# Token halves of 512 and 520 instead of 516 and 516 in a seven-product matrix scheme

## The chip, the core and the metric

The kernel runs on one core of a Trainium2 chip. The metric is device time in microseconds from start to end of one execution. The core has a matrix engine (TensorE, PE in the profile), three engines for elementwise work (VectorE, DVE; ScalarE, ACT; GpSimd, POOL) and a queue engine that issues transfers (SyncE, SP). Matmul results go to PSUM, eight banks of 512 fp32 numbers per partition, from which VectorE or ScalarE takes them.

## The reference

One layer of a decoder trunk for 1024 prompt tokens and 8 sample tokens that share the weights, 1032 tokens in all, width 1024:

```python
x = x + concat(pool_mixer(a), conv_mixer(glu)) @ w_out
x = x + cross_attn(rmsnorm(x, g_attn), mk, mv, w_q, w_o)
h = rmsnorm(x, g_ffn)
x = x + (silu(h @ w_gate) * (h @ w_up)) @ w_down      # D_FF = 2816, 22 tiles of 128
```

and a final RMSNorm; the state of the pooling and of the convolution and the memory's keys and values go out too. The change is about the third line, the SwiGLU.

## The kernel before, in words

All tensors lie with channels on the 128 partitions and tokens along the free dimension: 512 even prompt tokens, 512 odd ones, then 8 samples. fp32 matmuls are made of three passes over a high and a low part of each operand (`PASSES`, `split`).

The two matrix products of the SwiGLU are done by a scheme with seven block products in place of eight. Its blocks halve the tokens, the input channels and the output channels. The token halves are `TH` = 516 wide. For stage one (`first_two`, `sixth`, `others`) the blocks A11, A12, A22 of the normalised input and the sums S1 to S4 are made once (`plain_block`, `sum_blocks`) and kept as `ab`; for each of 22 hidden tiles f the weights' blocks and sums are prepared (`gu_load`, `gate_prep`, `sums_prep`: tiles wG, wTa, wTb, wU) and seven products of 4 blocks x 3 passes follow, in this order: A11 and A12 with wG, S2 in between with wTa, S3 with wTa, S1 and A22 with wTb, S4 with wU. VectorE (A11: ScalarE) adds each product from PSUM into the four quarters of `su` (`plus`, `copy_sums`); S1's is added twice, the second time after A22's. Multiplying by the row factors `Rf`, the SiLU and the blocks of the hidden activations for stage two (`gated`, `times_value`, `combine`, `to_blocks`, stored in the DRAM buffer `hb`) follow.

Stage two is the down projection: for each of the blocks A11, S2, S3, S1, A22, A12, S4 four units (`p`), each a product of 11 hidden pairs x 3 passes (`down_block`, `down_weights`, `whole_unit`, `first_half_unit`); the last unit is cut into two column spans (`LAST_SPANS`, `last_units`, line 1647), so that the final norm of one can run under the other.

`product` (line 1287) issues the matmuls. Each block product is two matmuls per weight block, 258 columns each (`TQ`), and takes a place in PSUM: products number 0 and 1 of every three take two banks of a three-bank buffer (`mm`, two of them), number 2 takes two single-bank buffers (`ms`, two of them).

What sets the order of all this is `Program.order`: a list planner with a cost per task and engine, priorities in program order, and buffers that are given out as they come free. It fixes each engine's instruction list when the kernel is built; on the chip each engine goes through its list in order and waits where an operand or a buffer is not ready. Tasks with a choice of engine (`{"Pool": ..., "DVE": ...}`) are placed by it too.

Of the kernel before, what the change touches and what calls it, by code (L numbers as in the profile page):

```python
# [49 lines left out]
LAST_SPANS = ((516, 516), (0, 258), (258, 258))  # L50
# [196 lines left out]
def hybrid_step_kernel(ctx: ExitStack, tc: tile.TileContext, io):  # L247
# [228 lines left out]
    def rsqrt_rows(name, dst, dkeys, total, tkeys, ones, lo, width, at=None, more=None, direct=False):  # L476
# [12 lines left out]
        for o, n in parts:  # L489
# [6 lines left out]
            if direct:  # L496
# [296 lines left out]
    def windows(g):  # L793
# [86 lines left out]
    def layer_norm():  # L880
        y_all = [conv_keys(cg) for cg in range(4)]
        for o, n in SPANS:
            ps = ms_buf(f"mean_ps{o}")
            add({"PE": 0.1 + 0.0017 * n}, lambda e, ps=ps, o=o, n=n: e.matmul(ps[:, :n], ones_c, ysum[:, o : o + n], start=True, stop=True),
                [(ysum,)], [(ps,)])
            for cg in range(4):
                add({"DVE": dve(n)}, lambda e, cg=cg, ps=ps, o=o, n=n: e.tensor_tensor(
                    y2[cg // 2][:, cg % 2, o : o + n], y2[cg // 2][:, cg % 2, o : o + n], ps[:, :n], ALU.subtract),
                    [(ps,)] + y_all[cg], [("yc", cg, o)])
# [308 lines left out]
    def quarter(j, i, h):  # L1198
        return xa[j][:, i, h * TH : (h + 1) * TH]

    def plain_block(b, j, i, h):
        split(lambda p: block(b, j, p), lambda p: bkey(b, j, p), lambda: quarter(j, i, h), TH, [(xa[j], i, h)], gain=vcol(V_FFN, j + 4 * i))
# [84 lines left out]
    def product(weights, wkeys, xs, steps=1):  # L1287
# [11 lines left out]
        def bank(c):  # L1299
            return sums[0][0]()[:, c] if len(sums) == 1 else sums[c][0]()  # L1300

        def emit(e, js):
            for j in js:
                for p, (wi, xi) in enumerate(PASSES):
                    for c in range(2):
                        e.matmul(bank(c), weights(j, wi), xs[0](j, xi)[:, c * TQ : (c + 1) * TQ],  # L1306
                                 start=j == 0 and p == 0, stop=j == nj - 1 and p == 2)
# [7 lines left out]
    def from_sums(sums, engine, cost, emit, r, w):  # L1315
        for src, sl, key in sums:
            add({engine: cost(sl.stop - sl.start)}, lambda e, src=src, sl=sl: emit(e, src(), sl), [key] + r, w)

    def plus_sums(o, okey, a, akey, sums):

        from_sums(sums, "DVE", dve, lambda e, src, sl: e.tensor_tensor(as_banks(o(sl), src), src, as_banks(a(sl), src), ALU.add),  # L1321
                  [akey], [okey])
# [470 lines left out]
```

## Time and profile before

| | |
|---|---|
| Time, median of 3 runs | 1245.13 us (1244.81 to 1248.44) |
| Time of the profiled execution | 1247.23 us |
| Its span, first to last instruction | 1245.4 us, mean granted TensorE clock 0.991 |
| TensorE busy | 1207.4 us, 8892 matmuls |
| VectorE, ScalarE, GpSimd busy | 934.3, 500.5, 429.3 us |
| Output projection of the attention ends, stage one begins | about 556 us |
| Down projection begins | about 1008 us |

The profile gives one execution. A row of the page or of a view names line, engine, operation, out<-in, partitions x columns, count, busy time and mean length, and the idle time of the engine just before with what ended it. The length of a matmul is longer than its distance to the next, since matmuls overlap; the distance is what counts. "L1306" is the matmul of `product`, "L1321" the sum out of PSUM.

### The profile page before, as it was taken

What the parts mean: (1) busy time and instruction counts of PE and PEld (TensorE: products, weight loads), DVE (VectorE), ACT (ScalarE), POOL (GpSimd) and SP (SyncE); (2) the same over time, 40 slices, a digit from 0 to 9 for tenths busy, and PEclk for the clock granted to TensorE, in tenths of its full rate; (3) what the DMA queues carried; (4) which work ended last, traced back from release to release, by engine and by line L of the source; (5) the groups of instructions that cost most, each with busy time, mean ns of one, the idle gap of its engine ahead of it and who ended that gap; (6) DMA issues with size and microseconds to landing.
All of it is one profiled execution on the core that took longest, in us unless ns stands there. A gap on an engine that the chain in (4) does not pass through costs nothing.

```text
span 1245.4 us, 22115 instructions
## 1 busy us (share of the span) xinstructions
PE 1207.4 (97%) x8892; PEld 1187.1 (95%) x8892; DVE 934.3 (75%) x1510; ACT 500.5 (40%) x677; POOL 429.3 (34%) x375
## 2 busy tenths in 40 slices
PE   8999996999999989999999999999999999999996
PEld 8999985999999979998999999999999999999996
DVE  7899888757367786669997878878887687656653
ACT  6766658454223452444222222222222243334531
POOL 3578741022101002214544353334353333345100
PEclk9999997999999999999999999999999999999998
DMA  7447686744256664233554546454533498554632
GB/s 282 104 85 165 143 241 174 215 96 153 102 181 226 239 236 170 102 107 97 179 166 141 172 161 197 146 170 153 183 120 111 134 336 306 202 195 152 177 114 69
DMA packets 102422, 208.74 MB, mean 168 GB/s; under 512 B 10096, under 2 KB 53296, under 8 KB 101040
## 3 DMA queue, kind: packets, MB, share of 16 engines
q1 hardware_dynamic: 98720, 194.23, 46.1%
q0 software_dynamic: 3600, 13.11, 6.1%
q8 instruction: 70, 1.15, 0.4%
q14 instruction: 32, 0.26, 0.1%
HBM read 159.75 MB, written 47.55 MB: 166 GB/s over the span
## 4 chain that ended last, share of the span: by engine, by line
PE 74%; DVE 10%; issue 7%; DMA 5%; ACT 2%; POOL 2%; SPq 0%; DVEq 0%; POOLq 0%; ACTq 0%
PE pr L1306 46%; PE ps L460 12%; PE oa L460 4%; PE ob L460 4%; DVE cacc L679 2%; DMA raw<-in_w_v 2%; PE sc L1016 2%; PE pv L1074 2%; PE fd L1647 1%; DMA gr<-in_w_gu 1%; DVE su L1321 1%; POOL w L363 1%; DVE su L1347 1%; PE psg L460 1%; PE psv L460 1%
## 5 line engine op out<-in xcount | busy, mean ns | idle before, releaser
L1306 PE MATMUL pr<-hb,dw 128*128 128x258 f32 x1716 | 208.7, 284 | 0.0
L1306 PEld LDWEIGHTS pr<-hb,dw 128*128 128x128 f32 x1716 | 207.8, 190 | 0.2
L1321 DVE TENSOR_TENSOR su<-pr,su 128x258 f32<-128x258 f32 (+1 forms) x204 | 109.5, 557 | 64.5 <-PE pr L1306 63.2
L1306 PE MATMUL pr<-ab,wG 128*128 128x258 f32 x1056 | 134.4, 283 | 2.6 <-DVE su L1321 1.8
L1306 PE MATMUL pr<-ab,wTa 128*128 128x258 f32 x1056 | 134.0, 283 | 0.0
L1306 PEld LDWEIGHTS pr<-ab,wG 128*128 128x128 f32 x1056 | 129.8, 189 | 3.4 <-ACT wU L352 2.4
L1306 PE MATMUL pr<-ab,wTb 128*128 128x258 f32 x1056 | 130.8, 283 | 1.1 <-DVE su L1321 1.1
L1306 PEld LDWEIGHTS pr<-ab,wTa 128*128 128x128 f32 x1056 | 130.1, 189 | 0.0
L1306 PEld LDWEIGHTS pr<-ab,wTb 128*128 128x128 f32 x1056 | 128.6, 190 | 1.3 <-DVE su L1321 1.3
L460 PE MATMUL ps<-xop,w 128*128 128x344 f32 x720 | 114.1, 320 | 0.5 <-DMA w<-in_w_in 0.5
L460 PEld LDWEIGHTS ps<-xop,w 128*128 128x128 f32 x720 | 113.3, 188 | 0.7 <-DMA w<-in_w_in 0.7
L460 PE MATMUL ps<-xq,w 128*128 128x344 f32 x576 | 94.8, 321 | 0.0
L460 PE MATMUL po<-oo,w 128*128 128x344 f32 x576 | 91.0, 320 | 0.4 <-DVE oo L1079 0.4
L460 PEld LDWEIGHTS po<-oo,w 128*128 128x128 f32 x576 | 90.7, 188 | 0.7 <-DVE oo L1079 0.7
L460 PEld LDWEIGHTS ps<-xq,w 128*128 128x128 f32 x576 | 90.7, 188 | 0.1
L679 DVE SCALAR_TENSOR_TENSOR cacc<-glu,vec,cacc 128x511 f32<-128x511 f32 (+14 forms) x116 | 77.0, 740 | 0.0
L352 ACT ACTIVATE wTa<-ta 128x1024 fp32r<-128x1024 f32 x22 | 23.4, 1064 | 110.9 <-DVE ta L1265 98.6
L1306 PE MATMUL pr<-ab,wU 128*128 128x258 f32 x528 | 67.1, 283 | 0.0
L352 ACT ACTIVATE dw<-dr 128x1024 fp32r<-128x1024 f32 (+1 forms) x36 | 33.0, 923 | 82.6 <-PE pr L1306 72.3
L1306 PEld LDWEIGHTS pr<-ab,wU 128*128 128x128 f32 x528 | 65.0, 190 | 0.0
L352 ACT ACTIVATE w<-raw 128x1024 fp32r<-128x1024 f32 (+2 forms) x32 | 29.4, 922 | 86.4 <-issue 38.6
L1347 DVE TENSOR_TENSOR su<-su,Rf 128x516 f32<-128x516 f32 x73 | 62.8, 863 | 1.5 <-ACT su L1354 0.6
(301 smaller groups left out, 2132.3 us busy)
## 6 DMA issues: line engine op xcount, KB each, us to landing
gr<-in_w_gu SPq DMA_DIRECT2D x44, 512.0 KB, 4.0
hs<-hb SPq DMA_DIRECT2D x35, 516.0 KB, 5.2
hb<-su SPq DMA_DIRECT2D x11, 1032.0 KB, 5.0
ds<-in_w_dn SPq DMA_DIRECT2D x22, 512.0 KB, 3.4
td<-ds SPq DMA_DIRECT2D x88, 128.0 KB, 2.1
dr<-td SPq DMA_DIRECT2D x16, 704.0 KB, 5.4
dr<-in_w_dn SPq DMA_DIRECT2D x24, 320.0 KB, 5.0
spcache_k<-in_cache_k SPq DMA_DIRECT2D x12, 512.0 KB, 4.8
```

Source lines behind the costliest of these rows:

```text
L352: e.activation(dst(0), src(), AF.Copy, scale=1.0 if gain is None else gain)
L363: e.tensor_tensor(dst(1), src(), f32(dst(0)), ALU.subtract)
L460: e.matmul(ps[:, c, :CW], w[:, wi, cols], x[:, xi, c * CW : (c + 1) * CW], start=first and p == 0, stop=last and p == 2)
L679: e.scalar_tensor_tensor(acc[h][:, n:], src[:, : HALF - n], w, acc[h][:, n:], ALU.mult, ALU.add)
L1016: e.matmul(bank()[:, i * NMEM : (i + 1) * NMEM], qop[2 * h + dt][:, qi, tt * P : (tt + 1) * P], kk[:, ki, 2 * (h % 2) + dt], start=(dt == ...
L1074: e.matmul(ps[:, c], v[:, vi, m, col : col + P], pT[h][m][:, pi, sl], start=(m == 0 and p == 0), stop=(m == 1 and p == 2))
L1306: e.matmul(bank(c), weights(j, wi), xs[0](j, xi)[:, c * TQ : (c + 1) * TQ], start=j == 0 and p == 0, stop=j == nj - 1 and p == 2)
L1321: from_sums(sums, "DVE", dve, lambda e, src, sl: e.tensor_tensor(as_banks(o(sl), src), src, as_banks(a(sl), src), ALU.add), [akey], [okey])
L1347: add({"Pool": pool_tt(TH), "DVE": dve(TH)}, lambda e: e.tensor_tensor(o(), o(), b(), ALU.mult), r + [(su[f], q)], [(su[f], q)], lock=True)
L1647: e.matmul(view(), weights(j, wi), moving(j, xi)[:, sl], start=j == 0 and n == 0, stop=j == PAIRS - 1 and n == 2)
```

## The change

The token halves become 512 and 520 wide: the first holds the even prompt tokens, the second the odd ones and the 8 samples. Blocks that hold only the first half (A11, A12, and S4, whose samples would be nothing) are 512 wide, the others (A22, S1, S2, S3) 520. A 512-wide product is one matmul per weight block into one single-bank buffer (`ms`); a 520-wide one is two of 260 into a three-bank buffer (`mm`). The ring of three places is gone: the width decides. Sums of blocks run over 512 columns, and the 8 samples' columns, which the first half does not have, are handled apart: cleared (`no_samples`), negated (`negate`), or split from S1 (S2's samples). The planner's costs for the two kinds of product are new. The transfers to and from `hb` are 512 or 520 columns wide. `LAST_SPANS` becomes (512, 520), (0, 256), (256, 256).

For the longer rows, memory is taken from two small tiles: `ones_c` (1/512) is dropped, the convolution's norm uses `ones_d` (1/1024) with a factor of -2 or `of=2`, and the sample scores `ssc` share the buffer `cnt`, so that `s_scores` comes after the pooling's `mean`.

```diff
-LAST_SPANS = ((516, 516), (0, 258), (258, 258))
+LAST_SPANS = ((512, 520), (0, 256), (256, 256))
...
-TH = T // 2
-TQ = TH // 2
+HALF_AT, HALF_WIDTH = (0, SEQ // 2), (SEQ // 2, SEQ // 2 + NS)
+TW = HALF_WIDTH[1]
 A12, A22, S4, S1, A11, S2, S3 = range(7)
+WIDTH = {A12: HALF_WIDTH[0], S4: HALF_WIDTH[0], A11: HALF_WIDTH[0], A22: TW, S1: TW, S2: TW, S3: TW}
...
-    ssc = const.tile([P, HEADS, 2, NS], F32, name="ssc")
+    ssc = cnt
...
-                    y2[cg // 2][:, cg % 2, o : o + n], y2[cg // 2][:, cg % 2, o : o + n], ps[:, :n], ALU.subtract),
+                    y2[cg // 2][:, cg % 2, o : o + n], ps[:, :n], -2.0, y2[cg // 2][:, cg % 2, o : o + n], ALU.mult, ALU.add),
...
+        split(lambda p: block(S2, j, p)[:, HALF_WIDTH[0] :], lambda p: bkey(S2, j, p) + ("samples",),
+              lambda: whole(S1)()[:, HALF_WIDTH[0] :], NS, [key(S1)], gain=-1.0)
...
-    def product(weights, wkeys, xs, steps=1):
+    def product(weights, wkeys, xs, width, steps=1):
...
-        if i % 3 < 2:
-            t = mm_buf(f"pr{i}", 2)
-            sums = [(lambda: t[:, :, :TQ], slice(0, TH), (t,))]
-        else:
-            sums = [(lambda t=t: t[:, :TQ], slice(c * TQ, (c + 1) * TQ), (t,)) for c, t in enumerate([ms_buf(f"pr{i}_{c}") for c in range(2)])]
...
+        banks = 1 if width <= 512 else 2
+        n = width // banks
+        t = mm_buf(f"pr{i}", 2) if banks == 2 else ms_buf(f"pr{i}")
+        sums = (t, width, n)
 
         def emit(e, js):
             for j in js:
                 for p, (wi, xi) in enumerate(PASSES):
-                    for c in range(2):
-                        e.matmul(bank(c), weights(j, wi), xs[0](j, xi)[:, c * TQ : (c + 1) * TQ],
+                    for c in range(banks):
+                        e.matmul(t[:, c, :n] if banks == 2 else t[:, :n], weights(j, wi), xs[0](j, xi)[:, c * n : (c + 1) * n],
                                  start=j == 0 and p == 0, stop=j == nj - 1 and p == 2)
...
-            add({"PE": 0.1195 * 6 * len(js)}, lambda e, js=js: emit(e, js),
-                wkeys + [k for j in js for k in xs[1][j]], [k for _, _, k in sums])
+            add({"PE": (0.231 if banks == 1 else 0.242) * 3 * len(js)}, lambda e, js=js: emit(e, js),
+                wkeys + [k for j in js for k in xs[1][j]], [(t,)])
...
+    def no_samples(o, okeys):
+        add({"Pool": 0.08}, lambda e: e.memset(o(), 0.0), [], okeys)
...
+            if negate:
+                e.tensor_scalar(o(tail), b(tail), -1.0, 1.0, ALU.mult, ALU.mult)
```

The planner's lists change with it. TensorE where stage one begins, before, from the last matmul of the output projection (`po7`); `pr` is a product's place in PSUM, with the product's number in program order (`pr0` and `pr1` are A11 and A12 of tile 0, `pr4` and `pr5` its S2 and S3), `ab4`, `ab0` and `ab5` are A11, A12 and S2, `Rf_ps` are the column sums for the row factors, which read the sum of squares `xss2`:

```order
L460 MATMUL po7_5134<-oo7_4405,w52_5046 128x344 x9
L1306 MATMUL pr0_5237<-ab4_0_4637,wG0_5144 128x258 x12
L1306 MATMUL pr0_5237<-ab4_1_4972,wG0_5144 128x258 x6
L1306 MATMUL pr1_5267<-ab0_0_4681,wG0_5144 128x258 x12
L1306 MATMUL pr0_5237<-ab4_1_4972,wG0_5144 128x258 x6
L1306 MATMUL pr1_5267<-ab0_1_5062,wG0_5144 128x258 x6
L491 MATMUL Rf_ps0_5300<-xss2_4628,ones_d_72 128x512
L491 MATMUL Rf_ps512_5305<-xss2_4628,ones_d_72 128x512
L491 MATMUL Rf_ps1024_5310<-xss2_4628,ones_d_72 128x8
L1306 MATMUL pr1_5267<-ab0_1_5062,wG0_5144 128x258 x6
L1306 MATMUL pr4_5326<-ab5_0_4744,wTa0_5208 128x258 x12
L1306 MATMUL pr4_5326<-ab5_1_5156,wTa0_5208 128x258 x6
```

The same place in the changed kernel:

```order
L459 MATMUL po7_5138<-oo7_4402,w52_5049 128x344 x9
L1315 MATMUL pr4_5247<-ab5_0_4738,wTa0_5214 128x260 x12
L1315 MATMUL pr4_5247<-ab5_1_5160,wTa0_5214 128x260 x6
L490 MATMUL Rf_ps0_5283<-xss2_4625,ones_d_72 128x512
L490 MATMUL Rf_ps512_5288<-xss2_4625,ones_d_72 128x512
L490 MATMUL Rf_ps1024_5293<-xss2_4625,ones_d_72 128x8
L1315 MATMUL pr0_5298<-ab4_0_4634,wG0_5148 128x512 x6
L1315 MATMUL pr0_5298<-ab4_1_4995,wG0_5148 128x512 x6
L1315 MATMUL pr1_5324<-ab0_0_4678,wG0_5148 128x512 x6
L1315 MATMUL pr1_5324<-ab0_1_5065,wG0_5148 128x512 x6
L1315 MATMUL pr4_5247<-ab5_1_5160,wTa0_5214 128x260 x6
L1315 MATMUL pr5_5356<-ab6_0_4741,wTa0_5214 128x260 x12
```

18 matmuls of S2 stand ahead of the factor sums, where 42 of A11 and A12 stood.

VectorE in tile 14 of stage one, before, from the sum of S2 (`pr99`) on; `pr100` is A12's product, `pr101` S3's (two single banks), `pr102` S1's, `pr103` A22's; `ds` belongs to the down projection's weights, `gr`, `ta`, `tb` to the next tiles' weights:

```order
L1321 TENSOR_TENSOR su14_8639<-pr99_8611,su14_8639 128x516
L1321 TENSOR_TENSOR su14_8639<-pr100_8647,su14_8639 128x516
L1347 TENSOR_TENSOR su14_8639<-su14_8639,Rf_5342 128x516
L363 TENSOR_TENSOR wG15_8705<-gr15_0_8375,wG15_8705 128x1024
L1347 TENSOR_TENSOR su14_8639<-su14_8639,Rf_5342 128x516
L1321 TENSOR_TENSOR su14_8639<-pr101_0_8679,su14_8639 128x258
L1321 TENSOR_TENSOR su14_8639<-pr101_1_8680,su14_8639 128x258
L1321 TENSOR_TENSOR su14_8639<-pr102_8714,su14_8639 128x516
L1434 SCALAR_TENSOR_TENSOR ds17_8676<-ds17_8676 128x2x128
L1265 TENSOR_TENSOR tb16_8775<-gr16_1_8712,gr16_0_8636 128x512
L1265 TENSOR_TENSOR ta16_8778<-gr16_1_8712 128x512
L1265 TENSOR_TENSOR ta16_8778<-tb16_8775,gr16_1_8712 128x512
```

The same tile in the changed kernel:

```order
L1336 TENSOR_TENSOR su14_7993<-pr99_8043,su14_7993 128x520
L1336 TENSOR_TENSOR su14_7993<-pr100_8076,su14_7993 128x512
L1374 TENSOR_TENSOR su14_7993<-su14_7993,Rf_5334 128x512
L362 TENSOR_TENSOR wG15_8121<-gr15_0_7845,wG15_8121 128x1024
L1374 TENSOR_TENSOR su14_7993<-su14_7993,Rf_5334 128x512
L1336 TENSOR_TENSOR su14_7993<-pr101_8096,su14_7993 128x520
L362 TENSOR_TENSOR wTb15_8155<-tb15_7996,wTb15_8155 128x1024
L1336 TENSOR_TENSOR su14_7993<-pr102_8130,su14_7993 128x520
L1278 TENSOR_TENSOR ta16_8191<-gr16_1_8128 128x512
L1278 TENSOR_TENSOR ta16_8191<-tb16_8189,gr16_1_8128 128x512
L1458 TENSOR_TENSOR ds15_8160<-ds15_8160 128x2x128
L1336 TENSOR_TENSOR su14_7993<-pr103_8163,su14_7993 128x520
```

Each product has one sum, S3's is in one piece, and a weight split (wTb) now stands between the sums of S3 and S1.

More of the change, by code (lines that the diff above doesn't have):

```diff
@@ L820, in mean @@
             e.scalar_tensor_tensor(cur(), cur(), 1.0 / w, ab[:, ai], ALU.mult, ALU.subtract)
-        add({"DVE": dve(T) + 0.3}, mean, [ck, ak, (side, "pool", g)], [ck], lock=True)
+        add({"DVE": dve(T) + 0.3}, mean, [ck, ak, (side, "pool", g)] + [("ssc", g, m, half) for m in range(2) for half in range(2)], [ck], lock=True)
         dops[g] = op_r(f"dop{g}")
@@ L1181, in bkey, with bkeys @@
         return (ab[b][j // 2], j % 2, p)
+    def bkeys(b, j):
+        return [bkey(b, j, p) for p in range(2)] + ([bkey(b, j, p) + ("samples",) for p in range(2)] if b == S2 else [])
     def proj_o(n):
@@ L1198, in quarter @@
     def quarter(j, i, h):
[L1199 removed]
+        return xa[j][:, i, of_half(h)]
     def plain_block(b, j, i, h):
[L1202 removed]
+        split(lambda p: block(b, j, p), lambda p: bkey(b, j, p), lambda: quarter(j, i, h), HALF_WIDTH[h], [(xa[j], i, h)], gain=vcol(V_FFN, j + 4 * i))
     def sum_blocks(j):
@@ L1313, in product @@
-        return sums
[L1315 to L1321, printed above, removed]
+        for at in range(0, nj, -(-nj // steps)):
+            js = range(at, min(nj, at - (-nj // steps)))
+            add({"PE": (0.231 if banks == 1 else 0.242) * 3 * len(js)}, lambda e, js=js: emit(e, js),
+                wkeys + [k for j in js for k in xs[1][j]], [(t,)])
@@ new lines, in product, with from_sums @@
+        return sums
+    def from_sums(sums, width, engine, cost, emit, r, w):
+        t, have, n = sums
+        pieces = [(lambda: t[:, :width], slice(0, width))]
+        if have > 512:
+            pieces = [(lambda: t[:, :, :n], slice(0, have))]
+            if width < have:
+                pieces = [(lambda c=c: t[:, c, : min(n, width - c * n)], slice(c * n, min(width, (c + 1) * n))) for c in range(2)]
+        for src, sl in pieces:
+            add({engine: cost(sl.stop - sl.start)}, lambda e, src=src, sl=sl: emit(e, src(), sl), [(t,)] + r, w)
@@ new lines, in combine, with emit @@
+    def combine(o, okey, a, akey, b, bkey, width, op=ALU.add, negate=False):
+        n = HALF_WIDTH[0] if negate else width
+        sl, tail = slice(0, n), slice(n, width)
+        def emit(e):
+            e.tensor_tensor(o(sl), a(sl), b(sl), op)
+            if negate:
+                e.tensor_scalar(o(tail), b(tail), -1.0, 1.0, ALU.mult, ALU.mult)
+        more = 0.08 if negate else 0
+        add({"Pool": pool_tt(n) + 2 * more, "DVE": dve(n) + more}, emit, [akey, bkey], [okey], lock=True)
@@ L1334, in of_tokens @@
         return product(lambda j, p: w[:, p, col + j * P : col + (j + 1) * P], [(w, 0), (w, 1)],
-                       (lambda j, p: block(b, j, p), [[bkey(b, j, p) for p in range(2)] for j in range(4)]), steps)
+                       (lambda j, p: block(b, j, p), [bkeys(b, j) for j in range(4)]), WIDTH[b], steps)
     def part(f, q):
-        return lambda sl=slice(0, TH): su[f][:, q, sl]
-    def plus(f, q, q2, sums):
-        plus_sums(part(f, q2), (su[f], q2), part(f, q), (su[f], q), sums)
+        return lambda sl=slice(0, HALF_WIDTH[q % 2]): su[f][:, q, sl]
@@ L1345, in times, with plus @@
+    def plus(f, q, q2, sums, width):
+        plus_sums(part(f, q2), (su[f], q2), part(f, q), (su[f], q), sums, width)
     def times(f, q, b, r):
-        o = part(f, q)
-        add({"Pool": pool_tt(TH), "DVE": dve(TH)}, lambda e: e.tensor_tensor(o(), o(), b(), ALU.mult),
+        o, n = part(f, q), HALF_WIDTH[q % 2]
+        add({"Pool": pool_tt(n), "DVE": dve(n)}, lambda e: e.tensor_tensor(o(), o(), b(), ALU.mult),
             r + [(su[f], q)], [(su[f], q)], lock=True)
     def gated(f, q):
-        o, k, R = part(f, q), (su[f], q), (lambda: Rf[:, q * TH : (q + 1) * TH])
+        o, k, R, n = part(f, q), (su[f], q), (lambda: Rf[:, of_half(q)]), HALF_WIDTH[q]
@@ L1608, in run @@
                 x2_load(p)
-            sums = product(weights, wkeys, hidden(b), len(GROUPS) if (b, p) == (A11, 0) else 1)
+            sums = product(weights, wkeys, hidden(b), WIDTH[b], len(GROUPS) if (b, p) == (A11, 0) else 1)
             if b in (A11, S2):
@@ L1627, in run @@
         def run(weights, wkeys):
-            into(p, 2 * i, product(weights, wkeys, hidden(b)))
+            into(p, 2 * i, product(weights, wkeys, hidden(b), WIDTH[b]))
             square((1, 2), 2 * p + i, False)
```

119 lines of the change are left out of this document (61 added, 58 removed).

## The prediction

> **What bounds the kernel now.** I read the page's busy line and its chain first, to see which engine sets the end, then a table by stage, then the chain in order of time.
>
> ```profile
> PE 1207.4 (97%) x8892; PEld 1187.1 (95%) x8892; DVE 934.3 (75%) x1510; ACT 500.5 (40%) x677; POOL 429.3 (34%) x375
> PE 74%; DVE 10%; issue 7%; DMA 5%; ACT 2%; POOL 2%; SPq 0%; DVEq 0%; POOLq 0%; ACTq 0%
> ```
>
> TensorE is busy for 97% of the span. The change touches only what comes after the output projection of the attention, from 556 us on, so the table of that part decides:
>
> ```profile
> core 0: us, PE busy (x) PEld busy (x) DVE busy (x) ACT busy (x) POOL busy (x), PEclk, DMA share, GB/s
> 581.00:703.00 122.00, 121.49 (x1008) 121.26 (x1008) 106.83 (x157) 32.87 (x44) 57.13 (x37) 1.00 0.49 159
> 703.00:947.00 244.00, 242.52 (x2016) 242.34 (x2016) 197.25 (x295) 61.27 (x83) 101.45 (x76) 1.00 0.49 160
> 947.00:1008.00 61.00, 60.86 (x506) 60.89 (x507) 43.66 (x59) 17.81 (x25) 26.14 (x15) 1.00 0.48 150
> 1040.00:1200.00 160.00, 160.00 (x1320) 159.77 (x1319) 105.47 (x115) 65.06 (x74) 58.12 (x47) 1.00 0.55 178
> ```
>
> The first three rows are the stage of the 22 hidden tiles, the last is the down projection. TensorE is busy over 99% of both, at a granted clock of 1.00, while VectorE, the next engine, has 72 to 88% in the first stage (43.66 of 61; 106.83 of 122) and 66% in the second. So a matmul that gets cheaper shortens the span, as long as VectorE empties the banks in time. What one matmul costs is its start-to-start distance, which the chain gives for long unbroken runs:
>
> ```profile
> 268.31 45.20 PE ob L460 x288
> 351.18 1.42 PE sc L1016 x12
> ...
> 702.58 0.70 DVE su L1321
> 703.42 219.47 PE pr L1306 x1824
> ...
> 946.30 0.71 DVE su L1321
> 947.14 228.29 PE pr L1306 x1890
> ```
>
> At width 258 (line 1306) 447.76 us for 3714 matmuls, 120.6 ns each, so a product pays 241.1 ns for each pair of halves. At 344 it is 156.9 ns, at 256 it is 118.3 ns. Width 512 stands in the projection of the memory values and in the attention's values (PE in order of time: start, length, count):
>
> ```profile
> 160.72 22.27 PE L917 MATMUL vps<-w,memg 128*128 128x512 f32 x96
> 182.83 3.31 PE L843 MATMUL kps<-memg,w 128*128 128x256 f32 x26
> ...
> 425.49 2.96 PE L1074 MATMUL pv<-pT,vv 128*128 128x512 f32 x12
> 428.28 1.56 PE L1016 MATMUL sc<-kT,qo 128*128 128x256 f32 x12
> ```
>
> (182.83 - 160.72) / 96 = 230.3 ns and (428.28 - 425.49) / 12 = 232.5 ns, the same kind of accumulation into one bank, with new weights at every matmul.
>
> **The narrow products, the gain.** A11, A12 and S4 become one matmul of 512 in place of two of 258. Stage one has 22 tiles x 4 blocks x 3 passes = 264 pairs of each, 792 together. In the down projection there are 11 x 3 = 33 pairs a unit: four units of A11, three each of A12 and S4 (the fourth is the split last unit), 330 together. I take 231 ns, between the two rows and nearest to the longer run: 241.1 - 231 = 10.1 ns, times 1122 = **-11.3 us**. With 230.3 it is -12.1, with 232.5 it is -9.6.
>
> The Trainium skill, "TensorE: Matmul & The Clock Gate", section "Wait — 56ns, not 53.3ns?", puts a back-to-back matmul at its columns over 2.4 GHz plus about 2.5 ns; as an estimate from that page two of 258 are 220.0 ns and one of 512 is 215.8, a gain of 4.2 ns and -4.7 us in all. The rows do not agree with it at any width here (120.6 against 110.0, 230.3 against 215.8), so I go by the rows.
>
> **The wide products, the loss.** A22, S1, S2 and S3 go from 258 to 260: (4 x 264 + 4 x 132) pairs are 3168 matmuls. From 258 to 344 a column costs (156.9 - 120.6) / 86 = 0.42 ns, so two cost 0.84 and all **+2.7 us**. Bounds: nothing, if 258 already pays for 260; and 2.3 ns each, +7.3 us, if the step from 256 to 258 (118.3 to 120.6) goes on. I take the slope, since it spans more columns. The last unit's 132 matmuls shrink from 258 to 256: **-0.1** at the slope, -0.3 at the step.
>
> **The turn from the projection to stage one, a loss.** This is where TensorE's order moves: the factor sums (Rf) now stand behind 18 matmuls of S2 where 42 of A11 and A12 stood.
>
> ```profile
> 556.88 5.28 PE L1306 MATMUL pr<-ab,wG 128*128 128x258 f32 x42 [0.81 <-ACT wU L352]
> 562.00 1.88 PE L491 MATMUL Rf_ps<-xss,ones_d 128*128 128x512 f32 x4
> 564.35 0.39 PE L491 MATMUL Rf_ps<-xss,ones_d 128*128 128x8 f32 x2 [0.47 <-DVE Rf_m L500]
> 581.29 3.15 PE L1306 MATMUL pr<-ab,wTb 128*128 128x258 f32 x24 [1.08 <-DVE su L1321]
> ...
> 559.86 0.76 DVE L365 SCALAR_TENSOR_TENSOR ab<-xa,vec,ab 128x516 fp32r<-128x516 f32 x1 [0.60 <-POOL ab L354]
> 560.53 1.23 DVE L390 TENSOR_TENSOR xss<-xss,x2sq 128x1032 f32<-128x1032 f32 x1
> ```
>
> The last rows are VectorE's: the sum of squares is complete at 560.53 + 1.23 = 561.76, and its order ahead of that is unchanged. TensorE will be through its 18 matmuls at 556.88 + 18 x 0.121 = 559.1 and then stand until about 561.9: **+2.8 us**. GpSimd now clears the samples' columns of two buffers ahead of wU and that block; if that delays them, it is up to 0.5 us more. The wait at 581.29 (1.08 us of idle, 1.2 in start-to-start) should go, **-1.2**: the wide bank that the second product with wTb needs is then that of S3, and its sum stands ahead of the second operation on ta in VectorE's order, where before it stood behind it. If it stays, that term is 0.
>
> **The ring of banks, a small gain.** Before, products went round three places, two pairs of banks and one pair of single banks, whatever the product. S1's place is held until its second sum, which stands behind A22's, and A11 of the next tile comes round to it one product (2.9 us) after A22 ends:
>
> ```profile
> 703.42 2.76 PE L1306 MATMUL pr<-ab,wG 128*128 128x258 f32 x21 [0.63 <-DVE su L1321]
> ...
> 942.97 0.69 DVE L1265 TENSOR_TENSOR tb<-gr,gr 128x512 f32<-128x512 f32 x1 [2.10 <-DMA gr<-in_w_gu]
> 945.51 2.08 DVE L1321 TENSOR_TENSOR su<-pr,su 128x258 f32<-128x258 f32 x4
> 947.14 3.12 PE L1306 MATMUL pr<-ab,wG 128*128 128x258 f32 x24 [1.20 <-DVE su L1321]
> ```
>
> At 942.97 VectorE had stood 2.10 us for a weight load, and the sums queued behind it held TensorE. Now A11 takes a single bank, and S1's pair is next wanted by the next tile's S2, after S4 and A11: 5.5 us. Both waits go, **-1.8 us**. What is late next is A22: its pair is S3's, free once S3's sum is done, one product (2.9 us) after S3 ends. By VectorE's order the sum of S3 follows the sum of A12, a multiplication by Rf, the split of wG and a second multiplication. Their durations, and the distance between starts, from one tile:
>
> ```profile
> 813.16 0.76 DVE L1321 TENSOR_TENSOR su<-pr,su 128x258 f32<-128x258 f32 x2 [2.00 <-PE pr L1306]
> 813.96 0.70 DVE L1347 TENSOR_TENSOR su<-su,Rf 128x516 f32<-128x516 f32 x1
> 814.57 1.22 DVE L363 TENSOR_TENSOR wG<-gr,wG 128x1024 fp32r<-128x1024 f32 x1
> 815.71 0.69 DVE L1347 TENSOR_TENSOR su<-su,Rf 128x516 f32<-128x516 f32 x1
> 816.31 0.69 DVE L1321 TENSOR_TENSOR su<-pr,su 128x516 f32<-128x516 f32 x1
> ```
>
> From the start of A12's sum to the end of S3's these take 817.00 - 813.16 = 3.8 us; TensorE wants the bank two products after A12, 5.8 us. That leaves 2 us in a tile that goes as this one. But the page's mean of that multiplication is longer than 0.70:
>
> ```profile
> L1347 DVE TENSOR_TENSOR su<-su,Rf 128x516 f32<-128x516 f32 x73 | 62.8, 863 | 1.5 <-ACT su L1354 0.6
> ```
>
> so some tiles go slower, and I allow **+0.8 us** for a few late sums over 22 tiles, between nothing and +4.
>
> **Costs at nothing.** A pair of half sums holds VectorE for 0.80 us (813.16 to 813.96), a whole one is 0.69 long, so the single banks give VectorE time. New are some 60 operations on 8 columns: negations, the clearing of the samples on GpSimd, the split of S2's samples. The nearest row:
>
> ```profile
> L354 POOL TENSOR_SCALAR oo<-os 128x8 fp32r<-128x8 f32 x8 | 4.2, 520 | 30.5 <-DVE spcache_v L1113 28.4 <-PE ps L460 1.2 <-PE pt L1055 0.9
> ```
>
> They lie in the idle time of VectorE and GpSimd in the table; without that cover 60 at 0.52 us would be 31 us. Transfers change by a few bytes a row, the DMA share being about 0.5. The mean's factor -2 and the shared buffer for the sample scores lie in the mixer and the attention, before 556 us, where TensorE's order is the same.
>
> **Sum.** -11.3 + 2.7 - 0.1 + 2.8 - 1.2 - 1.8 + 0.8 = **-8.1 us** on the profiled span of 1245.4, so 1237.3; that execution's own time is 1247.2, 1.8 above its span and 2.1 above the median of the runs. From the median, 1245.1 - 8.1 = **1237.0 us**. All best ends: -12.1 + 0 - 0.3 + 2.8 - 1.2 - 1.8 + 0 = -12.6, 1232.5. All worst: -9.6 + 7.3 - 0.1 + 3.3 + 0 + 0 + 4 = +4.9, 1250.0.
>
> **Rivals.** *The narrow matmul saves too little* (no change). If 512 columns in this stage cost what two rows of 256 do, 236.6 ns, a pair saves 4.5 ns, -5.0 us, and with the other terms (+3.2) the time is 1243.3. For it: at 256 and 258 the cost hardly depends on there being two instructions. Against: both rows of 512 are below 233 ns. The skill's page above comes to nearly this (by its 4.2 ns, 1243.6 as an estimate).
>
> *The wide matmul is dearer* (about -0.3%). With 2.3 ns a matmul the loss is 7.3 and the time 1241.6. For it: the step from 256 to 258. Against: the 258-to-344 slope, which reaches 512 within 5 ns of its rows.
>
> *A22 waits for S3's sum at every tile* (slower). The place is VectorE's queue at the first product with wTb. It decides once S3's sum ends more than 2.9 us after S3; each further microsecond, in 22 tiles, is 22 us, so 1 us late gives 1237 + 22 = 1259. For it: two wide places instead of three, and VectorE at 88% in the first tiles. Against: 2 us of slack in the tile above, and fewer operations for VectorE.
>
> **How the numbers follow.** A difference below 0.3% (3.7 us) cannot be told from none here. The forecast has 0.68, the dear wide matmul 0.12 (half of it beyond the bound), the small saving 0.12, the late S3 sum 0.08 (of which 0.01 would still end level). So faster 0.74, level 0.19, slower 0.07. The range goes from 1232 (near all best ends) to 1242.5, which takes in the dear wide matmul and leaves out about 2 in 10.
>
> **What would show it.** Right: runs of line 1315 at 512 near 231 ns and at 260 near 121.5 ns from start to start; an idle of 2 to 3 us before the factor sums near 559; no wait of the next tile's A11 on a sum of VectorE. Wrong: 512 near 236 or 260 near 123; or repeated idle before the second product with wTb, ended by VectorE's sum, which would sink the forecast.

## The result: slower, and where the time went

The changed kernel takes 1252.55 us (median of 19 runs, 1244.46 to 1261.15) beside 1247.74 us (19 runs, 1244.01 to 1250.06) of the kernel before in the same comparison. The ratio is 1.0041, 95% interval 1.0025 to 1.0057: slower, where 1237 was forecast and the range ended at 1242.5. The profiled execution took 1248.25 us (span 1246.5, granted clock 0.992), near the low end of its spread. The busy line and the chain's shares on its page:

```profile
PE 1198.3 (96%) x7770; PEld 1125.7 (90%) x7770; DVE 953.8 (77%) x1490; ACT 497.9 (40%) x668; POOL 421.6 (34%) x397
PE 67%; DVE 17%; DMA 8%; issue 3%; ACT 3%; POOL 1%; SPq 1%; DVEq 0%; ACTq 0%; POOLq 0%
```

The table by stage, with the columns that the prediction shows:

```profile
581.00:703.00 122.00, 119.79 (x810) 110.34 (x809) 110.32 (x150) 27.90 (x36) 51.49 (x43) 1.00 0.48 160
703.00:947.00 244.00, 241.23 (x1594) 221.12 (x1593) 208.71 (x278) 62.03 (x79) 92.65 (x79) 1.00 0.45 150
1040.00:1200.00 160.00, 156.42 (x1174) 149.73 (x1173) 104.57 (x111) 64.60 (x76) 64.26 (x46) 0.99 0.58 192
```

TensorE has 9.1 us less to do, as hoped, but it now stands 2.2 us in the first of these stages (0.5 before), 2.8 in the second (1.5) and 3.6 in the third (none). In the chain VectorE holds 17% where it held 10%: sums have come onto the path. TensorE's instructions in order of time show one tile that waits and the next, which does not:

```profile
662.84 2.93 PE L1315 MATMUL pr<-ab,wG 128*128 128x512 f32 x12
665.61 3.03 PE L1315 MATMUL pr<-ab,wTa 128*128 128x260 f32 x24
...
674.13 3.03 PE L1315 MATMUL pr<-ab,wTb 128*128 128x260 f32 x24
678.31 3.14 PE L1315 MATMUL pr<-ab,wTb 128*128 128x260 f32 x24 [1.15 <-DVE su L1336]
...
695.38 5.92 PE L1315 MATMUL pr<-ab,wTb 128*128 128x260 f32 x48
701.13 2.96 PE L1315 MATMUL pr<-ab,wU 128*128 128x512 f32 x12
```

The rates are good: (665.61 - 662.84) / 12 = 231 ns at 512 columns, (701.13 - 695.38) / 48 = 119.8 ns at 260. But at 678.31 A22, the second product with wTb, waits for VectorE's sum of S3. From 637 us on it does so in nine tiles, nearly every second one, for 0.37 to 1.32 us beyond the usual distance, 7.5 us together; the page's group of these matmuls has its idle by that name:

```profile
L1315 PE MATMUL pr<-ab,wTb 128*128 128x260 f32 x1056 | 132.6, 283 | 6.0 <-DVE su L1336 6.0
```

(The idle is less than the 7.5, which count from start to start.) VectorE's list there (line 1336 sums a product, 1374 multiplies by Rf, 362 is the low part of a weight), in the tile that waits and in the next:

```profile
671.46 0.69 DVE L1336 TENSOR_TENSOR su<-pr,su 128x512 f32<-128x512 f32 x1 [1.98 <-PE pr L1315]
672.18 0.69 DVE L1374 TENSOR_TENSOR su<-su,Rf 128x512 f32<-128x512 f32 x1
672.79 2.06 DVE L362 TENSOR_TENSOR wG<-gr,wG 128x1024 fp32r<-128x1024 f32 x1
674.78 2.87 DVE L1374 TENSOR_TENSOR su<-su,Rf 128x512 f32<-128x512 f32 x1
677.57 0.68 DVE L1336 TENSOR_TENSOR su<-pr,su 128x520 f32<-128x520 f32 x1
...
692.71 0.69 DVE L1336 TENSOR_TENSOR su<-pr,su 128x512 f32<-128x512 f32 x1 [1.33 <-PE pr L1315]
693.44 0.69 DVE L1374 TENSOR_TENSOR su<-su,Rf 128x512 f32<-128x512 f32 x1
694.05 1.22 DVE L362 TENSOR_TENSOR wG<-gr,wG 128x1024 fp32r<-128x1024 f32 x1
695.18 0.69 DVE L1374 TENSOR_TENSOR su<-su,Rf 128x512 f32<-128x512 f32 x1
695.78 0.69 DVE L1336 TENSOR_TENSOR su<-pr,su 128x520 f32<-128x520 f32 x1
```

The order is the same, but two instructions last 2.06 and 2.87 us in place of 1.22 and 0.69. What differs is GpSimd, which splits wTb in the one tile and not in the other:

```profile
672.25 1.54 POOL L353 TENSOR_SCALAR wTb<-tb 128x1024 fp32r<-128x1024 f32 x1 [2.49 <-DMA hb<-su]
673.87 3.23 POOL L362 TENSOR_TENSOR wTb<-tb,wTb 128x1024 fp32r<-128x1024 f32 x1
```

GpSimd ends at 677.10, and VectorE's multiplication, begun at 674.78, ends 0.55 us later, almost its whole usual length: it stood until GpSimd was through. GpSimd is held in the same way: its subtraction, 2.40 us long in e6 below, took 3.23 here beside VectorE's wG, which had begun first. S3 ends at 674.13 and the wide bank is wanted 24 matmuls (2.9 us) later. In the quiet tile the sum ends 1.1 us after S3 (696.47 - 695.38), in the waiting one 4.1 us after (678.25 - 674.13).

Two more places. At the turn into stage one the column sums for Rf stand behind 18 matmuls of S2; and in the down projection the final norm's column sums (`fin_ps`, single banks) and the narrow products wait for each other:

```profile
556.16 2.40 PE L1315 MATMUL pr<-ab,wTa 128*128 128x260 f32 x18 [0.84 <-DVE xa L1199]
561.06 1.98 PE L490 MATMUL Rf_ps<-xss,ones_d 128*128 128x512 f32 x4 [2.50 <-DVE xss L389]
...
1173.76 0.60 PE L493 MATMUL fin_ps<-fsq,ones_d 128*128 128x260 f32 x2
1176.42 9.44 PE L1315 MATMUL pr<-hb,dw 128*128 128x512 f32 x33 [2.05 <-DVE x L1336]
1186.64 0.71 PE L490 MATMUL fin_ps<-fin,ones_d 128*128 128x260 f32 x2 [0.78 <-DVE x L1336]
1187.19 0.60 PE L493 MATMUL fin_ps<-fsq,ones_d 128*128 128x260 f32 x2
1188.53 3.72 PE L1315 MATMUL pr<-hb,dw 128*128 128x512 f32 x15 [0.74 <-DVE fin_m L499]
...
1173.98 1.69 DVE L362 TENSOR_TENSOR dw<-dr,dw 128x1024 fp32r<-128x1024 f32 x2 [0.65 <-ACT dw L351]
1175.59 0.68 DVE L1336 TENSOR_TENSOR x<-pr,x 128x512 f32<-128x512 f32 x1
```

`fin_ps` holds one of the two single banks, the previous narrow product (ended at 1173.3) the other until its sum, which stands behind two weight splits on VectorE (the last two rows). The 33 matmuls from 1176.42 take 9.4 us, where 33 x 0.231 are 7.6: eight of them, from 1177.7 to 1181.1, run at about 420 ns. The three waits and the slow stretch are 2.3 + 1.0 + 1.0 + 1.5 = 5.8 us.

### The profile page after: what moved, and what is told of

It reads as the page before. It is cut to its first block, busy times and chain, and to the rows that moved or that the text cites. A ratio compares the mean times of both kernels' runs of the same rounds, so it can differ in the third digit from the quotient of the medians.

```text
span 1246.5 us, 19894 instructions
## 1 busy us (share of the span) xinstructions
PE 1198.3 (96%) x7770; PEld 1125.7 (90%) x7770; DVE 953.8 (77%) x1490; ACT 497.9 (40%) x668; POOL 421.6 (34%) x397
## 4 chain that ended last, share of the span: by engine, by line
PE 67%; DVE 17%; DMA 8%; issue 3%; ACT 3%; POOL 1%; SPq 1%; DVEq 0%; ACTq 0%; POOLq 0%
PE pr L1315 36%; PE ps L459 11%; PE po L459 7%; PE oa L459 4%; PE ob L459 4%; DVE su L1336 2%; DVE cacc L678 2%; DMA raw<-in_w_v 2%; DVE su L1374 1%; PE sc L1015 1%; PE fd L1678 1%; DMA spcache_k<-in_cache_k 1%; DMA gr<-in_w_gu 1%; DVE wG L362 1%; DVE spcache_k L1112 1%
## 5 line engine op out<-in xcount | busy, mean ns | idle before, releaser
L1315 PE MATMUL pr<-hb,dw 128*128 128x260 f32 (+1 forms) x1386 | 205.6, 310 | 3.2 <-DVE x L1336 2.5
L1315 PE MATMUL pr<-ab,wTb 128*128 128x260 f32 x1056 | 132.6, 283 | 6.0 <-DVE su L1336 6.0
L1315 PE MATMUL pr<-ab,wTa 128*128 128x260 f32 x1056 | 133.5, 282 | 1.5 <-DVE xa L1199 0.8
L1315 PE MATMUL pr<-ab,wG 128*128 128x512 f32 x528 | 128.8, 393 | 0.2 <-DVE Rf_m L499 0.2
L1336 DVE TENSOR_TENSOR su<-pr,su 128x520 f32<-128x520 f32 (+1 forms) x154 | 106.0, 689 | 28.1 <-PE pr L1315 26.9
L1315 PEld LDWEIGHTS pr<-ab,wG 128*128 128x128 f32 x528 | 97.8, 188 | 21.2 <-DVE Rf_m L499 0.3
L1374 DVE TENSOR_TENSOR su<-su,Rf 128x512 f32<-128x512 f32 (+1 forms) x75 | 69.7, 930 | 1.3 <-ACT su L1381 0.5
L1315 PE MATMUL pr<-ab,wU 128*128 128x512 f32 x264 | 65.0, 395 | 0.0
L1336 DVE TENSOR_TENSOR x<-pr,x 128x520 f32<-128x520 f32 (+3 forms) x34 | 20.3, 628 | 55.0 <-PE pr L1315 47.7
L351 ACT ACTIVATE wG<-gr 128x1024 fp32r<-128x1024 f32 x21 | 22.3, 1062 | 96.9 <-PE pr L1315 87.6
```

Of the source, the lines that this page charges most:

```text
L351: e.activation(dst(0), src(), AF.Copy, scale=1.0 if gain is None else gain)
L1315: e.matmul(t[:, c, :n] if banks == 2 else t[:, :n], weights(j, wi), xs[0](j, xi)[:, c * n : (c + 1) * n], start=j == 0 and p == 0, stop=j ...
L1336: from_sums(sums, width, "DVE", dve, lambda e, src, sl: e.tensor_tensor(as_banks(o(sl), src), src, as_banks(a(sl), src), ALU.add), [akey], ...
L1374: add({"Pool": pool_tt(n), "DVE": dve(n)}, lambda e: e.tensor_tensor(o(), o(), b(), ALU.mult), r + [(su[f], q)], [(su[f], q)], lock=True)
```

## The experiments

Each run's time stands beside runs of the kernel before on the same chip. The profiled executions reach stage one at 555 to 559 us, so the profiles are compared from the first matmul of stage one to the end of the span: 688.5 us before, 690.3 after.

| run | median us | ratio to before, 95% interval | stage one to end, us |
|---|---|---|---|
| e1 changed kernel again | 1252.99 | 1.0062 (1.0049 to 1.0075) | 692.8 |
| e2 wTb's low part on VectorE | 1244.55 | 1.0000 (0.9988 to 1.0013) | 684.1 |
| e3 norms' sums in wide buffers | 1243.01 | 0.9980 (0.9967 to 0.9994) | 682.7 |
| e4 both | 1240.78 | 0.9959 (0.9946 to 0.9973) | 681.1 |
| e5 old ring, new halves | 1236.67 | 0.9938 (0.9917 to 0.9960) | 683.8 |
| e6 wTb's low part on GpSimd | 1250.65 | 1.0034 (1.0022 to 1.0047) | 690.8 |
| e7 before, wTb's low part on VectorE | 1246.91 | 1.0010 (1.0002 to 1.0019) | 688.3 |
| e8 e4, wG and first hb on VectorE too | 1238.18 | 0.9928 (0.9915 to 0.9941) | 678.0 |
| e9 e4, first hb on VectorE, negations on ScalarE | 1233.76 | 0.9897 (0.9882 to 0.9913) | 674.5 |
| e10 old ring again | 1237.31 | 0.9927 (0.9914 to 0.9940) | 678.4 |
| e11 old ring, wTb on VectorE, negations on ScalarE | 1241.68 | 0.9952 (0.9934 to 0.9971) | 683.6 |

**e1, the changed kernel again.** No edit.

> The changed kernel once more, unaltered, as the base of the other runs and for the profile of another execution. In its first profile A22 waits for the sum of S3 in nine tiles from 637 us on (0.37 to 1.32 us each, 7.5 us together), and in each of these GpSimd subtracts the low part of wTb (2.4 to 3.2 us) while VectorE does the low part of wG and a multiplication by Rf, which then last 2.06 and 2.87 us in place of 1.22 and 0.69. Theory one, the two engines slow each other: the waits stand again in the tiles where GpSimd has that subtraction, and in no others, 7 to 12 us together; time 1252 +- 2 us, before x 1.004. Theory two, the place in PSUM: with two wide places A22 is late whenever anything is late, so the waits also stand in tiles whose wTb is VectorE's. Theory three, chance of the one execution: the waits stand in other tiles, or are gone.

A22 waited in the same kind of tiles and in no other: the nine with GpSimd's wTb (0.05 to 2.60 us) and the last, where GpSimd subtracts low parts of hb (2.22 us), 7.9 us together. Theory one. The place is fixed, the size is not: it follows when GpSimd begins: 1.8 us before TensorE wants the bank it cost 2.60 us, 4.1 us before 1.01, 5.3 us before 0.05. (In the first profile, too, eight of the nine waits stand beside wTb, and the last, at 1001.9 us, beside low parts of hb.) This execution took 2.5 us longer than the first from stage one on, and two slow stretches make that up. After 2.54 us of idle the Rf sums ran at about half their rate, so that wG's next product began 9.4 us after the first matmul of the stage (8.0 in the first profile); and after the wait in the last tile:

```profile
1001.23 3.03 PE L1315 MATMUL pr<-ab,wTb 128*128 128x260 f32 x24
1006.32 4.59 PE L1315 MATMUL pr<-ab,wTb 128*128 128x260 f32 x24 [2.06 <-DVE su L1336]
```

The granted clock (the third number from the end) in a table of the two stretches:

```profile
560.00:580.00 20.00, 16.79 (x82) 12.92 (x82) 18.19 (x27) 13.14 (x19) 4.69 (x5) 0.91 0.34 108
1006.00:1014.00 8.00, 7.68 (x38) 7.12 (x39) 4.57 (x6) 3.19 (x6) 6.78 (x7) 0.79 1.11 299
```

The same 24 matmuls last 4.59 us in place of 3.03. Half rate for 3.4 of the 8 us would give 0.79, the clock of the second row.

**e2, the collision taken away.**

```diff
-        parts(Tb, lambda: tb[:], 1024, [(tb, 0), (tb, 512)])
+        parts(Tb, lambda: tb[:], 1024, [(tb, 0), (tb, 512)], True)
```

The new last argument, `quick`, leaves the low part to VectorE alone.

> The low part of wTb is always VectorE's; nothing else is altered, and VectorE's list in a tile keeps its order, with that subtraction (1.22 us) behind the sum of S3 in every tile where it stood in every second. Theory one (GpSimd's subtraction slows the two instructions ahead of S3's sum): the nine waits of A22 go, from 7.5 us to under 1; the multiplications by Rf fall from a mean of 0.93 us to about 0.75; the time falls by 7 us or a little more, to about 1245, and its spread over runs becomes narrower. Theory two (two wide places are too few whatever GpSimd does): VectorE has 1.22 us more in eleven tiles, so the waits stay or grow, and the time is 1252 or above.

Theory one: 8.4 us less, though VectorE is busier (958.4 us against 949.7). Of A22's waits 0.15 us is left in one tile and 2.88 in the last. The multiplication's mean fell from 957 (e1) to 817 ns, less than to the 750 expected, since other GpSimd work still meets it. The last tile's wait is the same collision with other names, low parts of hb on GpSimd and of dw on VectorE, and TensorE's next product runs slow there too:

```profile
990.98 0.92 DVE L1374 TENSOR_TENSOR su<-su,Rf 128x512 f32<-128x512 f32 x1
991.82 3.42 DVE L362 TENSOR_TENSOR dw<-dr,dw 128x1024 fp32r<-128x1024 f32 x1
995.16 2.85 DVE L1374 TENSOR_TENSOR su<-su,Rf 128x512 f32<-128x512 f32 x1
...
991.32 8.94 POOL L362 TENSOR_TENSOR hb<-hs,hb 128x1024 fp32r<-128x1024 f32 x3
...
998.68 4.67 PE L1315 MATMUL pr<-ab,wTb 128*128 128x260 f32 x24 [2.72 <-DVE su L1336]
```

**e3, the single banks freed of the norms.**

```diff
-            ps = ms_buf(f"{name}_ps{o}")
+            wide = name == "Rf" or direct
+            ps = mm_buf(f"{name}_ps{o}", 1) if wide else ms_buf(f"{name}_ps{o}")
```

> The column sums of the two norms (Rf at the turn into stage one, and the final norm's in the down projection) take a bank of a three-bank buffer in place of a single bank. TensorE's list at the turn again has A11 and A12 ahead of the Rf sums, as before the change; in the down projection its order is as in the changed kernel. Theory one (the narrow products and the norms' sums wait for each other's two single banks): the 2.66 us ahead of the Rf sums fall below 0.5, and the waits from 1176 to 1189 us (2.31, eight of 0.2, 0.95 and 1.00, about 5.9 us) below 1; the time falls by about 7 us, to 1245. Theory two (these waits are covered by VectorE's or the transfers' lateness just behind them): the named waits go, others stand behind them, and the time stays within 2 us of 1252.

Theory one, and more: 10.0 us less than e1. Ahead of the Rf sums 0.67 us of wait is left (2.70 in e1, and its stretch). The narrow product behind `fin_ps` now starts at once, and 33 matmuls end in 7.97 us:

```profile
1172.81 0.60 PE L495 MATMUL fin_ps<-fsq,ones_d 128*128 128x260 f32 x2
1173.05 7.97 PE L1317 MATMUL pr<-hb,dw 128*128 128x512 f32 x33
```

A22 still waits, 8.2 us in the nine tiles with more than 0.3 us each (1.72 of it in tile 2, where GpSimd has the low part of wTa in place of wTb). So these are two separate losses.

**e4, both edits.**

> Both edits of the two runs before: wTb's low part on VectorE, the norms' sums in three-bank buffers. If both theories one hold and their savings lie in different stages, they add: 1252 - 7 - 7 = 1238 us, 0.992 of the kernel before, which is about the forecast of the prediction (1237). If either edit only moves its wait, 1245 or above.

12.2 us less than e1, not 18.4: neither theory's time. What the norms gave at the two places stayed, and a wait of 0.73 us at 641; but TensorE now waits 2.41 us at 596 us, ahead of the first product with wTb in tile 1, which wants the bank of S2, and 1.3 us of stretch follow. GpSimd subtracts wG's low part there, a task that the planner gives it in the builds with the norms' wide sums. The last tile's 2.88 us of wait and 1.45 of stretch stayed.

**e5, the ring put back.**

```diff
-        t = mm_buf(f"pr{i}", 2) if banks == 2 else ms_buf(f"pr{i}")
+        ts = [mm_buf(f"pr{i}", banks)] if i % 3 < 2 else [ms_buf(f"pr{i}_{c}") for c in range(banks)]
```

> The halves stay 512 and 520, but a product's place in PSUM goes by its number again: numbers 0 and 1 of every three take a three-bank buffer, number 2 single banks (two for a 520-wide product, one for a 512-wide), so there are three wide places as before the change. The planner answers with more of GpSimd: 35 low parts of weights in place of 14, 12 of them wTb. Theory one (GpSimd's subtraction makes S3's sum late, and two wide places make TensorE pay for it): with the third place A22 no longer wants S3's bank, so the waits at the second product with wTb are under 1 us together although GpSimd subtracts more; A11 waits for S1's bank a few times again (about 2 us, as before the change); A11 and A12 stand ahead of the Rf sums again. Time 1252 - 7 - 3 + 2 = 1244 or a little below. Theory two (GpSimd's subtractions cost wherever the products lie): with 35 of them the time is 1252 or above.

Theory one, and lower than it said: 1236.67 us. With three wide places the new halves gain what was forecast for them, although GpSimd has 34 low parts of weights. Its profile is that of an execution of 1244.83 us, with one wait of A22 of 6.09 us in tile 1 (under 1 us was expected), 0.73 us at A11 and none of A22's after tile 1. The edit also makes the planner order the engines anew, so the third place was not changed alone.

**e6, more on GpSimd.** wTb's low part loses VectorE as a choice.

```diff
             lo["Pool"] = pool_tt(n)
+            if pool:
+                del lo["DVE"]
```

> The suspected cost doubled: the low part of wTb is always GpSimd's, 22 tiles in place of 9; VectorE has 1.22 us less in the other tiles. Theory one (VectorE's instructions on two SBUF operands stand while GpSimd subtracts): waits of A22 for S3's sum in more tiles than the nine, or longer ones, 10 to 18 us together, time 1255 to 1262. Theory two (VectorE has too much ahead of S3's sum): it has less now, so the waits shrink and the time falls below 1250.

Both theories' numbers missed: 1250.65 us, and A22 waits in six tiles, 6.5 us. The number of subtractions does not decide; whether one falls beside what stands ahead of S3's sum does. In most of the other tiles GpSimd begins after that sum. In four tiles in the middle of the stage the planner put that sum ahead of wG, and it passes while GpSimd subtracts:

```profile
718.19 0.70 DVE L1338 TENSOR_TENSOR su<-pr,su 128x520 f32<-128x520 f32 x1 [2.18 <-PE pr L1317]
718.80 2.24 DVE L364 TENSOR_TENSOR wG<-gr,wG 128x1024 fp32r<-128x1024 f32 x1
...
716.32 2.40 POOL L364 TENSOR_TENSOR wTb<-tb,wTb 128x1024 fp32r<-128x1024 f32 x1
```

The sum has one operand in PSUM and keeps its 0.70 us beside GpSimd. The instructions seen to be held up to here read both operands from SBUF; e8 adds one that reads a single operand there.

**e7, the same edit before the change.** As e2, in the kernel before.

> The kernel before the change with the one edit that took 8 us from the changed kernel: wTb's low part always VectorE's. Theory one (the late sum costs only where two wide places make A22 wait for S3's): before has three wide places and nothing of this wait, so it stays within 2 us of the kernel before. Theory two (GpSimd's subtraction costs by itself, in any ring): it falls by 5 to 8 us, and the edit says nothing on the change.

Theory one: 1246.91 us, 0.1% above before. With three wide places a late S3 sum costs nothing, so the edit has nothing to give.

**e8, the remaining collisions.** e4 with

```diff
-        parts(gu_w[f][0], lambda: rg[:], 1024, [(rg,)])
+        parts(gu_w[f][0], lambda: rg[:], 1024, [(rg,)], True)
...
-            split(lambda p, o=o: o[:, p], lambda p, o=o: (o, p), src, n * WIDTH[b], [key])
+            split(lambda p, o=o: o[:, p], lambda p, o=o: (o, p), src, n * WIDTH[b], [key], quick=b == A11)
```

> The changed kernel with both edits of the run that had them together, and two more of the same kind: the low parts of wG and of the first block of hidden activations are VectorE's too. In the run of both, three waits of A22 for S3's sum were left: at 596 us (2.41, GpSimd subtracts wG's low part from 589.15 to 592.11 while VectorE's multiplication by Rf lasts 2.88 us), at 641 (0.73) and at 1000.6 us (2.88, GpSimd subtracts parts of hb while VectorE's split of dw lasts 3.42 and a multiplication 2.85); behind the first and the last of them some 14 matmuls ran at about 1.8 times their distance, 1.3 and 1.5 us more. Theory one: both long waits and their slow stretches go, 8 us, time 1241 - 8 = 1233. Theory two (VectorE, now with five more subtractions near the end of stage one, is itself late for S3's sum there): the wait at 1000 us stays, about 1237.

Half of each theory. The last tile's wait is gone, against theory two. The one in tile 1 (as in e4 it is S1 that waits, for the bank of S2) grew to 4.52 us, against theory one: GpSimd has no wG there now, but two weight sums and a split for a later tile. Two rows of the split, VectorE and GpSimd:

```profile
593.97 2.30 DVE L1352 TENSOR_SCALAR su<-he 128x8 f32<-128x8 f32 x1
...
593.72 2.52 POOL L362 TENSOR_TENSOR wTa<-ta,wTa 128x1024 fp32r<-128x1024 f32 x1 [0.56 <-ACT wTa L351]
```

The change's own negation of eight columns, 0.16 us elsewhere, stood here for GpSimd's whole subtraction.

**e9, the best version.** e4 with the first block of hb on VectorE and

```diff
-            if negate:
-                e.tensor_scalar(o(tail), b(tail), -1.0, 1.0, ALU.mult, ALU.mult)
...
+        if negate:
+            add({"ACT": act(NS)}, lambda e: e.activation(o(tail), b(tail), AF.Copy, scale=-1.0), [bkey], [okey])
```

> The run of both edits, with the low parts of the first block of hidden activations on VectorE and the 22 negations of eight columns on ScalarE; wG's low parts may go to GpSimd again (it gets one). In the run before this one a negation of eight columns, 0.16 us elsewhere, lasted 2.30 us (593.97 to 596.27) while GpSimd subtracted a low part (593.72 to 596.24), and S3's sum stood behind it. Theory one (VectorE stands while GpSimd holds something the two share, whatever the size of VectorE's instruction): the wait at 1000 us stays away as in the run before; the one near 596 is set by what GpSimd does there and not by the negation, since the next instruction on two SBUF operands (ds, 0.41 us) then stands in its place; so 2.4 to 4.5 us are left there and the time is 1235 to 1238. Theory two (the negation itself is slow beside GpSimd): the wait near 596 falls below 1 us, and the time to 1233.

1233.76 us, ratio 0.9897, below what theory one allowed and near the time of theory two. But tile 1 kept 2.32 us, about what theory one said, and from there to the final norm TensorE never stands. What GpSimd does there is another thing than in e8, the low part of wG as in e4, beside a multiplication by Rf:

```profile
586.40 2.90 DVE L1375 TENSOR_TENSOR su<-su,Rf 128x520 f32<-128x520 f32 x1
...
585.80 2.94 POOL L362 TENSOR_TENSOR wG<-gr,wG 128x1024 fp32r<-128x1024 f32 x1 [0.42 <-ACT wG L351]
```

So this run does not show what the negation alone was worth. From the chain:

```profile
592.54 570.30 PE pr L1317 x3921
1162.83 0.44 PE fin_ps L492 x2
```

It beats the kernel before by 1.0%, and with it the changed one, whose ratios are 1.0041 and 1.0062.

**e10, the old ring again.** The same kernel as e5.

> The new halves with the old ring once more, unaltered: five of seven times were 1234.9 to 1237.0 us and two 1243.2 and 1244.8, and the profile was that of the slowest, with one wait of 6.09 us at 604 us (VectorE's sums behind two instructions that last 2.30 and 2.85 us beside GpSimd) and 1.9 us of stretched matmuls behind it. Theory one (these 8 us are the difference between the two groups of times): an execution near 1236 shows that wait below 1 us, and one near 1244 shows it again. Theory two: the fast executions have the same wait and differ elsewhere. The median: 1237, 0.994 of before.

Theory one as far as it was seen: in this execution of 1237.31 us the wait in tile 1 is 0.24 us (6.09 in that of 1244.83); none of the five times was near 1244, so the other half of the theory was not seen. A22 waits nowhere after tile 1. A11 waits once, 1.6 us ahead of 645, and from there the chain has one piece to 999 us, shortly before the down projection begins at 1003:

```profile
644.99 354.11 PE pr L1322 x2363
```

**e11, the old ring with wTb on VectorE.** The edits of e2, e5 and the negations of e9 together.

> The new halves with the old ring, wTb's low part on VectorE and the negations on ScalarE. Theory one (with three wide places a late sum of S3 costs nothing, so wTb's place does not matter, as in the kernel before): the median stays within 2 us of the old ring alone, 1235 to 1238; if the wait at 604 us goes with it (GpSimd then has 14 low parts of weights in place of 35), the slow times near 1244 go and the median is 1235. Theory two (GpSimd's subtractions cost in any ring): it falls by 5 us or more, to 1231.

Both numbers missed: 1241.68 us, 4.4 above e10. Its profile has no wait of A22 after tile 1 either, so wTb's place gives nothing in this ring; the loss is in tile 1 (3.88 us of wait, 2.6 of stretch), where the planner's new order again puts GpSimd beside VectorE. Why it falls there in some builds and executions and not in others stays open: it was not tried with the order of tile 1 alone changed.

## Why the prediction was wrong, point by point

**The narrow products** were right in mechanism and in what a matmul costs, and the gain is a little smaller than summed. In the traces the mean distance within runs on the same weights was 120.0 ns with wG and wU and 120.8 in the down projection before, and is 231.0, 232.8 and 231.7 ns after: 528 x 9.0 + 264 x 7.2 + 330 x 9.9 ns = 9.9 us saved, where 11.3 was forecast. The pooled 241.1 ns for a pair was too much for stage one.

**The wide products** were mis-sized: the sum had +2.7. 260 columns take 119.6 and 119.7 ns (wTa, wTb) and 120.0 ns (down projection), where 258 took 120.2, 120.2 and 120.8, so the term is -1056 x (0.6 + 0.5 + 0.8) ns = -2.0 us. Neither the slope nor the step went on. The rival of the dear wide matmul falls, and the one of the narrow product that saves too little.

**The turn** was right as a wait, 2.66 us against +2.8. What it left out is the stretch behind such an idle, 1.4 us in e1 (9.4 against 8.0). The wait at 581.29 went as said, and one of 0.8 us at 588 came.

**The ring** is the step that failed. A11's two waits went, -2.2 us (-1.8 forecast). But "what is late next is A22" was priced at +0.8, and it cost 7.5 to 7.9 us. The price was taken from one tile at 813 us. For such tiles the slack was right: 1.8 us here, 2 forecast. Every second tile is another kind, and the long mean of the multiplication (863 ns) was the sign of it; it was counted as "a few late sums", with nothing on what makes one long. The trace of before shows it, at a place where nothing waited for it. VectorE's subtraction for tb, usually 0.7 us long, beside GpSimd's low part of wTb:

```profile
697.67 2.06 DVE L1265 TENSOR_TENSOR tb<-gr,gr 128x512 f32<-128x512 f32 x1
...
696.79 2.39 POOL L363 TENSOR_TENSOR wTb<-tb,wTb 128x1024 fp32r<-128x1024 f32 x1 [6.79 <-ACT wTb L352]
```

The Trainium skill, "SBUF — State Buffer", section "SBUF: two separate sides", says why: VectorE and GpSimd share a pair of ports, and whichever begins first keeps it for its whole instruction; on VectorE's side that concerns instructions in a mode that uses both ports, or with two SBUF inputs against a GpSimd instruction that reads SBUF. The trace agrees: the multiplication of 0.69 us ended 0.55 us after GpSimd's 3.23, and the sums out of PSUM kept their 0.70.

The third rival named the place, A22 behind VectorE's queue, and the point from which it decides, 2.9 us after S3. Its price was wrong: not every tile but nine or ten, 0.8 us in the mean, and a chance of 0.07 for slower was too small. The runs say that the cost takes both halves of it: with GpSimd's subtraction moved away (e2) or with three wide places (before, e10) A22 waits 0.15 us at most in these tiles.

**Not in the sum at all:** the two single banks. The prediction saw what the narrow products leave (the third wide place) and not what they share: `fin_ps` stands in the same two banks, 5.8 us.

Put together from stage one on, against the kernel before: -9.9 - 2.0 + 2.7 - 0.4 (581 gone, 588 come) - 2.2 + 7.5 + 5.8 = +1.5; measured 690.3 - 688.5 = +1.8. Small items (the second matmul after each wait of A22 takes 0.1 us longer, 0.9 together; a wait of 0.6 us at 1031) would make it +3.0, so the account holds to about 1 us. Of the 9.9 us between the forecast's -8.1 and this, the ring is 6.7, the single banks 5.8 and the narrow products 1.4; the wide ones gave 4.7 back. That the medians differ by more, 4.8 us, fits the second execution (692.8), with its two slow stretches. Only these two executions of the changed kernel have a profile, so how often the stretches come is not shown.

**Costs at nothing.** The 21 negations on VectorE are 0.16 us each, 3.3 us under cover, as said; but one of them took 2.30 us in e8, when its cover was GpSimd's subtraction.

## What to carry to other kernels

Before an edit takes a buffer from a ring, look for the latest release in every kind of tile, not the typical one, and follow each long instruction of a kind that is usually short to what runs beside it on the other engines. An engine that is 34% busy can still hold up one on the path: VectorE's two-operand work and GpSimd's should not meet ahead of a sum that TensorE waits for. When a product moves to another kind of buffer, list everything else that takes that buffer, also in later stages.

## What the hardware showed that was not expected

- A matmul of 260 columns costs no more than one of 258 (119.6 to 120.0 ns against 120.2 to 120.8, on the same weights). The runs do not show why.
- After TensorE stood for about 2 us, matmuls often ran at 1.8 times their distance for about 3.4 us (1177.7 to 1181.1 us in the first profile, after 2.05 us), some 1.5 us more. In e10 an idle of 1.80 us was enough; in e1 one of 2.44 us, at 643, had no such stretch, nor had one of 2.15 in e9. After 3.72 us in e11 the stretch lasted 6.2 us. The Trainium skill, "TensorE: Matmul & The Clock Gate", section "What's actually happening", gives the half clock after an idle window of about 3.4 us; the runs show it after shorter ones, and a stretch as long as that window.
- GpSimd's hold is not shared by size: an eight-column VectorE instruction stood 2.30 us behind it.
